# Head sums of the RWKV bonus: float32 column strips beside the key norms in place of two full-array matmuls, spread by a load from DRAM

## The chip, the cores and the metric

The kernel runs on one NeuronCore of a Trainium2 chip. The metric is the device time of one execution in microseconds (us); each comparison is between runs of both kernels on one chip. The profile of one execution tells for each engine when each instruction ran. PE is TensorE (matmuls; PEld its weight loads), DVE is VectorE, ACT is ScalarE, POOL is GpSimd, SP is SyncE, which here only issues DMAs.

## The reference, cut to what matters

One layer with two branches that read the same normalised input: 16 RWKV-7 heads of 64 channels, and a short gated convolution; then one output projection and a final norm. There are 512 frames behind 16 meta tokens. The part that the change touches is the bonus of the RWKV branch, and beside it stands the norm of the keys:

```python
hn = _rmsnorm(h_res, norm_in_g[l])
P = hn @ w_in[l]                       # 2048 -> r, k, v, gates, low-rank inputs, convolution
...
kk = (k * k_k[l]).reshape(bsz, L, H, N)
kk = kk / jnp.maximum(jnp.linalg.norm(kk.astype(jnp.float32), axis=-1, keepdims=True), 1e-12)
k = k * (1.0 + (a - 1.0) * k_a[l])
...
y = _rwkv7_recurrence(...)             # S_t = S diag(w) - (S kk)(kk a)^T + v k^T, y = S r
yn = (yn * lnx_g[l] + lnx_b[l])        # per-head norm of y
bonus = jnp.sum(rh * kh * r_k[l], axis=-1, keepdims=True) * vh
y_a = (yn + bonus.reshape(bsz, L, D_RWKV)) * jax.nn.silu(g_r)
...
h_res = h_res + mix @ w_out[l]
```

So for each frame and head there is one sum over 64 channels of r k r_k, and this one number multiplies the 64 channels of v.

## The kernel before

**Two streams on PE.** Activations lie with 128 channels on the partitions and the frames along the free dimension; two heads (a *pair*) make one 128-channel tile, so there are eight pairs, numbered 0 to 7. The input projection is the generator `mains()`: one tile of 128 output channels after another (`k`, `r`, `v`, `g` for the pairs, `B`, `C`, `h`, `gc` for the convolution). Each weight quarter is split into a high and a low half (L151 on ACT, L152 on DVE, rows `w<-wr`), which lie in a ring of six buffers, and three matmul passes follow (`xh`, `xl` against the high half, `xh` against the low one): 24 matmuls of some 256 columns for most tiles (L353), 12 of 512 columns for `B` and `gc` (L368). All other work of PE, `prepare(i)` for a pair, `invert` for two pairs, `recur` for the recurrence, is woven into this stream by hand: `fill(ns)` runs the projection for as many nanoseconds of PE work (by a fixed rate per column) before the next piece. The order of PE is thus written out; for ACT, DVE, POOL and SP a scheduler makes the order when the program is built. A step handed to `later(ns, fn)` enters the program once the projection has run that much further. Each engine works its queue strictly in order.

**A pair.** `prepare(i)` makes the chunk operands `ar` and `bk`, then multiplies r in place by half of r_k and by the scaled keys (L735, out `r`). The key norms need sums over each head: `key_norms` (L786) squares k into `sq` (576 columns) and adds up over the 64 channels of a head by four matmuls with a 128x32 slice of the constant 0/1 matrix in `cs`. The four take a quarter of the columns each (144) and stand side by side in the array, by `tile_position=(0, 32*j)`, so that each writes 32 partitions of the PSUM bank `z[0]`; rows 0 to 15 of a strip are one head, 16 to 31 the other. They run as plain float32. ACT copies the strips out (L781, `n2`, shown as `n`), two DMAs store them (`sn`, L685), one DMA loads them back in another layout (`nd`), for the inversion of small triangular blocks that DVE does line by line (L855 to L888, tile `y`). `z` is the pair of banks that the next projection tile will use; in it stand also a first small product (`ar`, `bk`, L766), and in some pairs the second level of the inversion (L1007, L1025, L1029).

**The bonus before.** The product in `r` is split into a high half on ACT and a low half on DVE (`split`, L663: rows `rk_h` L665 and `rk_l` L666, 128x512), both are multiplied with a 128x128 matrix `ones` that adds within a head and at once copies the sum to all 64 partitions of the head (L820, L821, tile `zb`), ACT copies the result over `r` (L822), DVE multiplies it by v (L919), and SP stores it to `rbd[i]` for the end of the kernel (L920). The zero strip of the next v is written by POOL (L465) once v was read.

**The end.** After the projection (last tile `gc`), the output projection runs in 56 blocks of matmuls (`M`, `P`, `Q`, L1383) on split weights (`o`, `x`, `wo`, L1338 to L1352) and split activations (`S`, L1295); then come the final norm and the stores.

Of the kernel before, what the change touches and what calls it, by code (L numbers as in the profile page):

```python
# [9 lines left out]
F32 = mybir.dt.float32  # L10
F32R = mybir.dt.float32r
I32 = mybir.dt.int32
AF = mybir.ActivationFunctionType
ALU = mybir.AluOpType
# [4 lines left out]
P = 128  # L19
DM = 2048  # L20
KT = DM // P
SEQ = 512
META = 16
L = SEQ + META
CH = 64
NCH = SEQ // CH + 1
LP = NCH * CH
# [5 lines left out]
C_ID, C_GM, C_BM, C_ON = 0, 128, 384, 512  # L33
# [11 lines left out]
    tr=3200, lev=3000, cp=4200, out=1500, begin=19500, p=2900, u=2900, s=4200, mid=1000, last=3700, mix=2600,  # L45
# [44 lines left out]
def hymba_kernel(ctx: ExitStack, tc: tile.TileContext, xt, xtok, front, w_in, w_out, pv, lup, cst, msk, gf, out):  # L90
    nc = tc.nc
    ctx.enter_context(tc.manual_schedule(engines={mybir.EngineType.PE}))
    cp = ctx.enter_context(tc.tile_pool(name="cp", bufs=1))
    dp = ctx.enter_context(tc.tile_pool(name="dp", bufs=2, space=DRAM))
# [3 lines left out]
    cs = cp.tile([P, C_N], F32, name="cs")  # L98
# [6 lines left out]
    rbd = [dp.tile([P, SEQ], F32, tag=f"rbd{j}", name=f"rbd{j}", bufs=1) for j in range(NPAIR)]  # L105
# [6 lines left out]
    def col(off, i=0):  # L112
        return pvt[:, off + i : off + i + 1]
# [55 lines left out]
    xp = ph1.enter_context(tc.tile_pool(name="xp", bufs=1))  # L169
# [3 lines left out]
    rst = xp.tile([P, 4], F32, name="rst")  # L173
    rsx = cq.tile([P, 2 * META], F32, name="rsx")
    la = cq.tile([P, 2, L], F32R, name="la")
    ones = xp.tile([P, P], F32R, name="ones")
    omm = xp.tile([P, 33], F32, name="omm")
    hv = xp.tile([P, 6, 8], F32, name="hv")
    hl = cp.tile([P, 2, 8], F32, name="hl")
# [3 lines left out]
    pi = ph1.enter_context(tc.tile_pool(name="pi", bufs=1, space=PSUM))  # L183
# [5 lines left out]
    def tr(name, dt=F32):  # L189
        return cq.tile([P, LP], dt, tag="tr", name=name, bufs=5)  # L190
# [122 lines left out]
    with tc.issue_after(head):  # L313
        nc.vector.tensor_scalar(
            out=omm, in0=pvt[:, V_MU : V_MU + 33], scalar1=-1.0, scalar2=1.0, op0=ALU.mult, op1=ALU.add
        )
        for d, off in (
# [4 lines left out]
                out=d, in0=pvt[:, off : off + 8], scalar1=0.5, scalar2=None, op0=ALU.mult  # L322
            )
        nc.vector.tensor_scalar(
            out=hv[:, 4], in0=pvt[:, V_KA : V_KA + 8], scalar1=-0.5, scalar2=1.0, op0=ALU.mult, op1=ALU.add
        )

    nc.scalar.copy(ones, cs[:, C_BM : C_BM + P])
    FULL = ((0, 272), (272, L))
    TAIL = ((14, 272), (272, L))  # L330
    REAL = ((META, L),)
# [44 lines left out]
    def next_banks():  # L376
        what, i = plan[state["tile"] + 1]
        return [pm.tile([P, 512], F32, tag="main", name=f"ps_{what}{i}_{r}") for r in range(2)]
# [217 lines left out]
    def later(ns, fn):  # L596
        pending.append((clock[0] + ns, fn))
        pending.sort(key=lambda e: e[0])
# [16 lines left out]
    def fill(ns):  # L615
        while ns > 0:
            seen = len(ready)
            t = step()
            if t is None:
                return  # L620
            ns -= t
            if len(ready) > seen:
                ns += FW["evac"]
# [23 lines left out]
    def ahead():  # L647
        return tc.high_priority(offset=AHEAD)

    def c3(t):  # L650
        return t.rearrange("p (c s) -> p c s", s=CH)
# [7 lines left out]
        nc.vector.tensor_tensor(out=lo, in0=raw, in1=hi.bitcast(F32), op=ALU.subtract)  # L659
        return hi, lo  # L660

    def split(t, name, n):
        hi = tr(f"{name}_h", F32R)[:, 0:n]  # L663
        lo = tr(f"{name}_l", F32R)[:, 0:n]
        nc.scalar.copy(hi, t)  # L665
        nc.vector.tensor_tensor(out=lo, in0=t, in1=hi.bitcast(F32), op=ALU.subtract)  # L666
        return hi, lo

    heads = [(h, slice(64 * h, 64 * h + 64), slice(64 - 64 * h, 128 - 64 * h)) for h in range(2)]

    place = [(i % 2) * 4 + i // 2 for i in range(NPAIR)]
# [11 lines left out]
    def behind(dst, src):  # L683
        with tc.issue_after(state["dma"]):
            nc.sync.dma_start(dst, src)  # L685
# [5 lines left out]
    def second_level(z):  # L691
        return [t[:, 256:512].rearrange("p (q k s) -> p q k s", q=2, s=32) for t in z]

    def prepare(i):
# [22 lines left out]
            out=bk[:, :, 0], in0=c3(k), scalar=hv[:, 2, i : i + 1], in1=c3(te), op0=ALU.mult, op1=ALU.mult  # L717
# [3 lines left out]
            out=ta, in0=ta, scalar1=hv[:, 3, i : i + 1], scalar2=hv[:, 4, i : i + 1], op0=ALU.mult, op1=ALU.add  # L721
        )
        nc.vector.scalar_tensor_tensor(
            out=ar[:, :, 0], in0=c3(k), scalar=col(V_KK, i), in1=e1[:, :, 0:CH], op0=ALU.mult, op1=ALU.mult
# [6 lines left out]
        r = got["r", i]  # L731
        nc.vector.tensor_tensor(
            out=ar[:, 1:NCH, 1], in0=c3(r), in1=e1[:, 1:NCH, 1 : CH + 1], op=ALU.mult
        )
        nc.vector.scalar_tensor_tensor(  # L735
            out=r, in0=r, scalar=hv[:, 5, i : i + 1], in1=ta[:, CH:LP], op0=ALU.mult, op1=ALU.mult
        )

        sq = tr(f"sq{i}")
        nc.scalar.activation(sq, k, AF.Square, scale=col(V_KK, i))  # L740
        rh, rl = split(r, f"rk{i}", SEQ)
        fill(FW["gram_b" if p else "gram"] + FW["meta"].get(i, 0))

        late = state["step"] > 48
# [16 lines left out]

        def gram_meta():
            z = early or next_banks()
            norms = key_norms(z[0][:, 96 : 96 + NS]) if late else None
            for h, hs, ho in heads:
                nc.tensor.matmul(  # L766
                    z[h][:, 0:META],
                    bk[hs, 0, h : h + 2, :].rearrange("p a s -> p (a s)"),
                    ar[hs, 0, 0, 0:META],
                    start=True, stop=True,  # L770
                )
            norms = norms if late else key_norms(z[0][:, 96 : 96 + NS])
            if p and "levels" in state:
                state["out"] = state.pop("levels").pop(0)(second_level(z))
            with ahead():
                for h in range(2):
                    nc.vector.tensor_tensor(
                        out=gt[:, h, 0, 0:META], in0=z[h][:, 0:META], in1=gmask[:, h, 0:META], op=ALU.mult
                    )
            with ahead():  # L780
                nc.scalar.copy(n2, norms)  # L781
            if "out" in state:
                state.pop("out")()
            state["banks"] = z

        def key_norms(z):  # L786
            for j in range(4):
                nc.tensor.matmul(
                    z[32 * j : 32 * j + 32], cs[:, C_BM + 48 : C_BM + 80], sq[:, j * NS : (j + 1) * NS],
                    start=True, stop=True, tile_position=(0, 32 * j),  # L790
                )
            return z
# [11 lines left out]

        NS = LP // 4
        n2 = tr(f"n2{i}")[:, 0:NS]
        if late:
            gram_meta()
        za = [pz.tile([P, 4, P], F32, tag="tz", name=f"g{i}_1_{h}") for h in range(2)]
# [3 lines left out]
        if not late:  # L813
            gram_meta()
# [1 line left out]
        masked(zc, 5, 9)  # L816
        fill(FW["gram2"] - FW["meta"].get(i, 0))

        zb = pi.tile([P, SEQ], F32, tag="ser", name=f"zb{i}")
        nc.tensor.matmul(zb, ones[:, 0:P], rh, start=True, stop=False)  # L820
        nc.tensor.matmul(zb, ones[:, 0:P], rl, start=False, stop=True)  # L821
        nc.scalar.copy(r, zb)  # L822
        fill(FW["misc"])


# [4 lines left out]
        sg = dp.tile([SCR], F32, tag="sg", name=f"sg{i}")  # L830
        sn = dp.tile([2 * LP], F32, tag="sn", name=f"sn{i}")
        sx = scr_x[i % 2]

        def rows(t, h):
            return bass.AP(tensor=t.tensor, offset=t.offset + h * NCH * 4 * BLK, ap=[[CH, CH], [4 * BLK, NCH], [1, CH]])
# [3 lines left out]

        for h in range(2):  # L840
            behind(sn[h * LP : (h + 1) * LP].rearrange("(j s) -> j s", s=NS), n2[16 - 16 * h : P : 32])
        for h in range(2):
            behind(rows(sg, h), gt[64 * h : 64 * h + 64, h, :, 0:CH])
        NB = 8 * NCH
# [20 lines left out]
        def sub(x, r0, c0, dims):  # L865
            return bass.AP(tensor=x.tensor, offset=x.offset + r0 * 16 + c0, ap=[list(x.ap[0])] + dims)

        for m in (2, 4, 8):
            for b in range(16 // (2 * m)):
# [4 lines left out]
                    out=pq,  # L874
                    in0=sub(d, o, o + m, [[16, m], [0, m], [1, m]]),
                    in1=sub(y, o + m, o + m, [[0, m], [1, m], [16, m]]),
                    op=ALU.mult,
                )
                nc.vector.tensor_reduce(
                    out=tq.rearrange("p (i j) -> p i j", i=m), in_=pq, op=ALU.add, axis=AX.X  # L880
                )
                nc.vector.tensor_tensor(
                    out=pq,
                    in0=sub(y, o, o, [[16, m], [0, m], [1, m]]),
                    in1=bass.AP(tensor=tq.tensor, offset=tq.offset, ap=[list(tq.ap[0]), [0, m], [1, m], [m, m]]),
                    op=ALU.mult,
# [19 lines left out]
        for h, hs, ho in heads:  # L906
            for b in range(2):
                for a in range(2):
                    later(9000 + 900 * (4 * h + 2 * b + a), lambda h=h, b=b, a=a: nc.sync.dma_start(
                        bass.AP(  # L910
                            tensor=bd.tensor,
                            offset=bd.offset + (h ^ a) * (NCH - 1) * CH * NPAIR * P + place[i] * P + 64 * h + 32 * b,
                            ap=[[NPAIR * P, 32], [32 * NPAIR * P, 2 * NCH - 2], [1, 32]],
# [2 lines left out]
                    ))  # L916
        until("v", i)
        v = got["v", i]
        nc.vector.tensor_tensor(out=r, in0=r, in1=v[:, CH:LP], op=ALU.mult)  # L919
        later(12500, lambda: nc.sync.dma_start(rbd[i], r))  # L920
        fill(FW["v"])

        vs = cq.tile([P, NCH, CH], F32, tag="vs", name=f"vs{i}")
# [1 line left out]
        for b in range(4):  # L925
            for t in range(2):
                later(14000 + 1000 * (2 * b + t), lambda b=b, t=t: nc.sync.dma_start(
                    bass.AP(
                        tensor=vd.tensor,
                        offset=vd.offset + (64 * (1 - b // 2) + 32 * t) * NPAIR * CH + place[i] * CH + 32 * (b % 2),  # L930
                        ap=[[NPAIR * CH, 32], [P * NPAIR * CH, NCH], [1, 32]],
# [427 lines left out]
    def here(t, n):  # L1359
        return xa[t][:, n * 512 : (n + 1) * 512] if n < 2 else xb[n - 2][:, t]  # L1360
# [153 lines left out]
    z = {}  # L1514
# [55 lines left out]
    with tc.manual_schedule(engines={mybir.EngineType.DVE, mybir.EngineType.Activation, mybir.EngineType.Pool}):  # L1570
# [16 lines left out]
        for part in range(2):  # L1587
            cols = slice(256 * part, 256 * part + 256)
            for jj in range(8):
                hi, lo = right[(1, "M2", jj // 2), jj % 2]  # L1590
# [4 lines left out]
            h = here(1, 2)[:, cols]  # L1595
# [70 lines left out]
```

## Time and profile before

| | |
|---|---|
| three runs | 991.49, 991.8, 992.1 us; median 991.8 us |
| the profiled execution | 991.71 us in all, 989.6 us from the first to the last instruction |
| granted TensorE clock in it | 0.998 |
| PE busy | 980.0 us (99%) |
| DVE, ACT, POOL busy | 706.8 us (71%), 390.6 us (39%), 127.8 us (13%) |
| DMA | 176.91 MB, mean 179 GB/s |

Busy time is time with an instruction of the program in work. Matmuls are pipelined, and their ends are modelled: what a matmul costs PE is read from the start of one to the start of the next. A line number Lnnn is that of the kernel before. In rows that end on something like `[1.38 <-DMA nd<-sn]` the engine stood idle for 1.38 us until the landing of that DMA. Rows of SPq, and of ACTq where a DMA is named, are the issue of a DMA by that engine's queue, not the transfer. A mark `x8` counts instructions; a float32 matmul has two records.

### The profile page before, as it was taken

The page shows a single profiled execution, that of the slowest core. Times are in us where ns is not written, and L with a number is a line of the kernel's source. Part 1 is how long each engine was busy: PE and PEld are TensorE (multiplying, and loading weights), DVE is VectorE, ACT ScalarE, POOL GpSimd, SP SyncE. Part 2 cuts the span into 40 slices and gives each one's busy share as a digit, 9 for nine tenths or more (in the row PEclk, how much of TensorE's full clock was granted, in tenths as well). Part 3 has the DMA queues.
Part 4 walks back from the last instruction along what each step waited for, and adds up shares of the span by engine and source line. Part 5 has one row for each costly group of instructions (what it writes and reads, how often), then busy time and mean ns, then how long its engine had stood idle before and what let it go on. Part 6 is the DMA issues. An engine that isn't in the chain of part 4 may idle for free.

```text
span 989.6 us, 23395 instructions
## 1 busy us (share of the span) xinstructions
PE 980.0 (99%) x9511; PEld 907.5 (92%) x9511; DVE 706.8 (71%) x1413; ACT 390.6 (39%) x731; POOL 127.8 (13%) x242
## 2 busy tenths in 40 slices
PE   9999999999999999999999999999999999999996
PEld 9999999999998999998999998889889898788885
DVE  7777966578675779653778654365756697998896
ACT  7553432343322434322434323232323335446454
POOL 0110302112010111010111010011211102001001
PEclk9999999999999999999999999999999999999999
DMA  9526586246684375853275856999886697697554
GB/s 325 156 91 152 143 206 164 82 130 145 153 199 150 92 187 123 209 153 115 89 176 125 202 143 192 275 253 258 229 267 167 181 300 182 180 320 189 150 128 171
DMA packets 205532, 176.91 MB, mean 179 GB/s; under 512 B 138544, under 2 KB 168048, under 8 KB 205040
## 3 DMA queue, kind: packets, MB, share of 16 engines
q1 hardware_dynamic: 202832, 166.50, 60.2%
q0 software_dynamic: 2304, 8.39, 5.0%
q8 instruction: 75, 1.23, 0.5%
q10 hardware_dynamic: 288, 0.52, 0.1%
q14 instruction: 33, 0.27, 0.1%
HBM read 139.02 MB, written 36.35 MB: 177 GB/s over the span
## 4 chain that ended last, share of the span: by engine, by line
PE 95%; DVE 3%; ACT 1%; issue 1%; DMA 0%; DVEq 0%; POOL 0%; ACTq 0%
PE ps_v L353 9%; PE ps_h L353 9%; PE ps_C L353 9%; PE ps_g L353 9%; PE ps_B L368 9%; PE ps_gc L368 9%; PE ps_k L353 8%; PE ps_r L353 8%; PE M L1383 5%; PE P L1383 4%; PE Q L1383 2%; PE g L755 2%; PE ps_k L368 1%; PE ps_r L368 1%; PE ps_lora L368 1%; PE zy L1141 1%
## 5 line engine op out<-in xcount | busy, mean ns | idle before, releaser
L151 ACT CAST w<-wr 128x512 fp32r<-128x512 f32 x252 | 153.7, 619 | 285.1 <-PE ps_C L353 44.8
L152 DVE TENSOR_TENSOR w<-wr,w 128x512 fp32r<-128x512 f32 x252 | 174.8, 705 | 116.4 <-ACT w L151 115.5
L353 PE MATMUL ps_v<-xh,w 128*128 128x256 f32 (+2 forms) x512 | 84.0, 285 | 0.0
L368 PE MATMUL ps_B<-xh,w 128*128 128x512 f32 x256 | 83.4, 394 | 0.0
L353 PE MATMUL ps_h<-xh,w 128*128 128x256 f32 (+2 forms) x512 | 81.7, 281 | 0.0
L353 PE MATMUL ps_g<-xh,w 128*128 128x256 f32 (+2 forms) x512 | 81.4, 281 | 0.0
L368 PE MATMUL ps_gc<-xh,w 128*128 128x512 f32 x256 | 81.2, 392 | 0.0
L353 PE MATMUL ps_C<-xh,w 128*128 128x256 f32 (+2 forms) x512 | 80.8, 280 | 0.0
L353 PEld LDWEIGHTS ps_v<-xh,w 128*128 128x128 f32 x512 | 73.9, 188 | 0.3
L353 PE MATMUL ps_k<-xh,w 128*128 128x256 f32 (+1 forms) x448 | 73.4, 285 | 0.0
L353 PEld LDWEIGHTS ps_g<-xh,w 128*128 128x128 f32 x512 | 72.0, 189 | 0.6 <-issue 0.2
L353 PE MATMUL ps_r<-xh,w 128*128 128x256 f32 (+1 forms) x448 | 72.5, 280 | 0.0
L353 PEld LDWEIGHTS ps_h<-xh,w 128*128 128x128 f32 x512 | 72.1, 189 | 0.3
L353 PEld LDWEIGHTS ps_C<-xh,w 128*128 128x128 f32 x512 | 71.8, 189 | 0.2
L353 PEld LDWEIGHTS ps_k<-xh,w 128*128 128x128 f32 x448 | 64.7, 188 | 0.4
L353 PEld LDWEIGHTS ps_r<-xh,w 128*128 128x128 f32 x448 | 63.5, 189 | 0.4 <-issue 0.2
L353 PE MATMUL ps_h<-xl,w 128*128 128x256 f32 x256 | 57.3, 281 | 0.0
L368 PEld LDWEIGHTS ps_gc<-xh,w 128*128 128x128 f32 x256 | 47.8, 188 | 10.0
L368 PEld LDWEIGHTS ps_B<-xh,w 128*128 128x128 f32 x256 | 47.8, 188 | 9.7
L353 PE MATMUL ps_C<-xl,w 128*128 128x256 f32 x256 | 56.2, 280 | 0.0
L353 PE MATMUL ps_v<-xl,w 128*128 128x256 f32 x256 | 55.8, 278 | 0.0
L353 PE MATMUL ps_g<-xl,w 128*128 128x256 f32 x256 | 55.4, 278 | 0.0
(382 smaller groups left out, 2144.5 us busy)
## 6 DMA issues: line engine op xcount, KB each, us to landing
wr<-in_w_in_dram SPq DMA_DIRECT2D x126, 512.0 KB
ct<-opd SPq DMA_DIRECT2D x72, 192.0 KB
wo<-in_w_out_dram SPq DMA_DIRECT2D x24, 512.0 KB
x<-in_w_out_dram POOLq DMA_DIRECT2D x16, 512.0 KB, 5.6
opd<-ar SPq DMA_DIRECT2D x8, 576.0 KB
opd<-gt SPq DMA_DIRECT2D x16, 288.0 KB
bd<-bt SPq DMA_DIRECT2D x64, 64.0 KB
bw<-bd SPq DMA_DIRECT2D x16, 256.0 KB
```

What stands on the lines that cost most here:

```text
L151: nc.scalar.copy(hi, rq)
L152: low[q] = eng.tensor_tensor(out=lo, in0=rq, in1=hi.bitcast(F32), op=ALU.subtract).ins
L353: nc.tensor.matmul(ps[r][:, 0 : b - a], ww[:, k * P : (k + 1) * P], xx[:, kt, a:b], start=(kt == 0 and n == 0), stop=(kt == KT - 1 and n = ...
L368: nc.tensor.matmul(ps[r], ww[:, w], xx[:, kt, a:b], start=(kt == 0 and n == 0), stop=(kt == KT - 1 and n == 2))
L755: nc.tensor.matmul(z[h][:, c - c0], bk[hs, c, h : h + 2, :].rearrange("p a s -> p (a s)"), ar[hs, c].rearrange("p a s -> p (a s)"), start= ...
L1141: nc.tensor.matmul(zy[e][hs if e else ho, k], t[hs, o : o + CH], x, start=(n == 0), stop=(n == 2))
L1383: nc.tensor.matmul(bank[s], left(prod, jj, m, s), w, start=(jj == 0 and n == 0), stop=(jj == 7 and n == 2))
```

## The change

The bonus is added up in the way of the key norms. Right behind the four matmuls on `sq` stand four on `r` (128 columns each, float32, the same 128x32 slice of `cs`, the same four strips), which write the other bank, `z[1]`. ACT copies these strips (128x128, tile `nb`) behind the norms. On ACT's own queue two DMAs store the 2 x 512 sums to DRAM (`sb`), and a third loads them back so that every partition of a head gets the 512 sums of its head, straight into `r` (256 KB in SBUF from 4 KB in DRAM). The product with v comes when the projection has run 14.5 us further (`later(14500, ...)`), the store to `rbd` after 17.5 us instead of 12.5. The split of `r`, the matrix `ones` and the two full-array matmuls go.

```diff
-    nc.scalar.copy(ones, cs[:, C_BM : C_BM + P])
...
         sq = tr(f"sq{i}")
         nc.scalar.activation(sq, k, AF.Square, scale=col(V_KK, i))
-        rh, rl = split(r, f"rk{i}", SEQ)
...
             z = early or next_banks()
-            norms = key_norms(z[0][:, 96 : 96 + NS]) if late else None
+            if late:
+                norms, bonus = sums_of(z)
...
-            norms = norms if late else key_norms(z[0][:, 96 : 96 + NS])
+            if not late:
+                norms, bonus = sums_of(z)
...
             with ahead():
                 nc.scalar.copy(n2, norms)
+                nc.scalar.copy(nb, bonus)
...
-        def key_norms(z):
+        def sums_of(z):
+            return head_sums(z[0][:, 96 : 96 + NS], sq, NS), head_sums(z[1][:, 96 : 96 + P], r, P)
+
+        def head_sums(z, x, n):
             for j in range(4):
                 nc.tensor.matmul(
-                    z[32 * j : 32 * j + 32], cs[:, C_BM + 48 : C_BM + 80], sq[:, j * NS : (j + 1) * NS],
+                    z[32 * j : 32 * j + 32], cs[:, C_BM + 48 : C_BM + 80], x[:, j * n : (j + 1) * n],
                     start=True, stop=True, tile_position=(0, 32 * j),
                 )
             return z
...
+        nb = tr(f"nb{i}")[:, 0:P]
...
-        zb = pi.tile([P, SEQ], F32, tag="ser", name=f"zb{i}")
-        nc.tensor.matmul(zb, ones[:, 0:P], rh, start=True, stop=False)
-        nc.tensor.matmul(zb, ones[:, 0:P], rl, start=False, stop=True)
-        nc.scalar.copy(r, zb)
         fill(FW["misc"])
...
+        sb = dp.tile([2 * SEQ], F32, tag="sb", name=f"sb{i}")
...
+        for h in range(2):
+            later(1000, lambda h=h: nc.scalar.dma_start(
+                sb[h * SEQ : (h + 1) * SEQ].rearrange("(j s) -> j s", s=P), nb[16 * h : P : 32]
+            ))
+        later(7000, lambda: nc.scalar.dma_start(r, bass.AP(tensor=sb.tensor, offset=sb.offset, ap=[[SEQ, 2], [0, CH], [1, SEQ]])))
...
-        nc.vector.tensor_tensor(out=r, in0=r, in1=v[:, CH:LP], op=ALU.mult)
-        later(12500, lambda: nc.sync.dma_start(rbd[i], r))
+        later(14500, lambda: nc.vector.tensor_tensor(out=r, in0=r, in1=v[:, CH:LP], op=ALU.mult))
+        later(17500, lambda: nc.sync.dma_start(rbd[i], r))
```

What that makes of the order, at three places (the number at a tile's end is that of its buffer; line numbers of the changed kernel are a few lower). PE at pair 4, before, where the bonus of the pair stands amid the projection tile `ps_k`:

```order
L353 MATMUL ps_k_0_4653<-xl,w_4431 128x256
L353 MATMUL ps_k_0_4653<-xh,w_4431 128x256 x2
L353 MATMUL ps_k_0_4653<-xl,w_4431 128x256
L353 MATMUL ps_k_0_4653<-xh,w_4431 128x256
L820 MATMUL zb_4808<-rk_h,ones 128x512
L821 MATMUL zb_4808<-rk_l,ones 128x512
L353 MATMUL ps_k_0_4653<-xh,w_4431 128x256
L353 MATMUL ps_k_0_4653<-xl,w_4431 128x256
```

PE at pair 4 in the changed kernel, at the key norms (`sq`), some 8 us earlier in the stream:

```order
L1006 MATMUL ps_k_0_4655<-xm_4191,gt_3489 32x32 x2
L1006 MATMUL ps_k_1_4656<-xm_4191,gt_3489 32x32 x2
L784 MATMUL ps_k_0_4655<-sq_4567,cs 32x144 x4
L784 MATMUL ps_k_1_4656<-r_4544,cs 32x128 x4
L757 MATMUL ps_k_0_4655<-ar_4393,bk_4394 128x16
L757 MATMUL ps_k_1_4656<-ar_4393,bk_4394 128x16
```

The two rows of `zb` are gone from the projection; one row of four strips stands behind that of the norms, and the rows around it are as before.

ACT at pair 5, before: the copy of the norms, casts of weights, the copy of `zb`:

```order
L781 COPY n_5321<-ps_g_0_5342 128x144
L151 CAST w_5280<-wr_5275 128x512
L151 CAST w_5312<-wr_5310 128x512
L822 COPY r_5121<-zb_5454 128x512
L151 CAST w_5315<-wr_5310 128x512
```

ACT at pair 5 in the changed kernel:

```order
L773 COPY n_5325<-ps_g_0_5347 128x144
L774 COPY nb_5326<-ps_g_1_5348 128x128
L837 DMA sb_5488<-nb_5326 4x128 x2
L151 CAST w_5284<-wr_5279 128x512
L840 DMA r_5128<-sb_5488 128x1x512
L151 CAST w_5316<-wr_5314 128x512
L151 CAST w_5319<-wr_5314 128x512
```

Three DMA issues stand between the casts, the third with one cast between it and the stores that it reads; in pairs 2, 4 and 6 it stands right behind the stores.

DVE at pair 5, before: the product with v stands behind two low halves of weights, ahead of the reading of the tile `ps_g`:

```order
L152 TENSOR_TENSOR w_5280<-wr_5275,w_5280 128x512
L152 TENSOR_TENSOR w_5312<-wr_5310,w_5312 128x512
L919 TENSOR_TENSOR r_5121<-r_5121,v_5261 128x512
L404 TENSOR_TENSOR pr_g_5533<-ps_g_0_5283,rs 128x256
L403 TENSOR_TENSOR ex<-ps_g_1_5284,rst 128x4
```

DVE at pair 5 in the changed kernel:

```order
L152 TENSOR_TENSOR w_5284<-wr_5279,w_5284 128x512
L918 TENSOR_TENSOR r_5128<-r_5128,v_5265 128x512
L152 TENSOR_TENSOR w_5316<-wr_5314,w_5316 128x512
L402 TENSOR_TENSOR pr_g_5539<-ps_g_0_5287,rs 128x256
L401 TENSOR_TENSOR ex<-ps_g_1_5288,rst 128x4
```

In spite of the later entry into the program, the product stands at nearly the same place of DVE's queue (here one low half earlier), and now it reads what a load brings. Elsewhere on DVE the low half `rk_l` is gone from each pair and small steps of the inversion have changed places with their neighbours; on SP the store `rbd<-r` stands a few DMAs later.

More of the change, by code (lines that the diff above doesn't have):

```diff
@@ L175, in hymba_kernel @@
     la = cq.tile([P, 2, L], F32R, name="la")
-    ones = xp.tile([P, P], F32R, name="ones")
     omm = xp.tile([P, 33], F32, name="omm")
@@ L660, in lora_up @@
         return hi, lo
[L662 to L667, printed above, removed]
     heads = [(h, slice(64 * h, 64 * h + 64), slice(64 - 64 * h, 128 - 64 * h)) for h in range(2)]
```

## The prediction

> **What bounds the kernel now.** I read the page first, then the chain of work that ended last, then PE's own waits.
>
> ```profile
> PE 980.0 (99%) x9511; PEld 907.5 (92%) x9511; DVE 706.8 (71%) x1413; ACT 390.6 (39%) x731; POOL 127.8 (13%) x242
> PE 95%; DVE 3%; ACT 1%; issue 1%; DMA 0%; DVEq 0%; POOL 0%; ACTq 0%
> ...
> PE pwarm L202 <- DVE cold L199: 1.0, 1, 1.0
> PE M L1383 <- DVE o L1352: 0.3, 1, 0.3
> ```
>
> The first row is busy time, the second the chain by engine, the last two all waits of PE that the trace names: 1.3 us in the whole run, one at its start, one in the output projection. PE is not merely busy, it is never kept waiting in the stretch where the eight pairs are prepared (84 to 547 us, by the rows below). So there a microsecond of PE work removed is a microsecond won, and work on DVE, ACT or SP counts only if it makes PE wait.
>
> How far PE is from waiting shows in who waits for it:
>
> ```profile
> ACT w L151 <- PE ps_C L353: 44.8, 23, 5.0
> DVE w L152 <- ACT w L151: 118.5, 89, 4.7
> ...
> 104.19 16.39 PE ps_g L353 x141
> ```
>
> The casts of weights wait mostly until PE gives a buffer of the ring back, and DVE waits for the casts. The last row, of the chain, gives 16.39 / 141 = 0.116 us a matmul, so a quarter of 24 lasts 2.8 us; with six buffers full, five quarters or some 14 us of weights lie ready. I take 10 us as the usual lead.
>
> **What goes from PE.** PE around `zb` in pair 7, then the removed work by line:
>
> ```profile
> 545.88 0.40 PE L353 MATMUL ps_g<-xh,w 128*128 128x256 f32 x2
> 546.12 0.39 PE L820 MATMUL zb<-rk_h,ones 128*128 128x512 f32 x1
> 546.35 0.39 PE L821 MATMUL zb<-rk_l,ones 128*128 128x512 f32 x1
> 546.58 0.28 PE L353 MATMUL ps_g<-xl,w 128*128 128x256 f32 x1
> ...
> L665 ACT CAST rk_h<-r x8: 620/621/624, 76.6 to 529.7; 128x512 fp32r<-128x512 f32 x8
> L666 DVE TENSOR_TENSOR rk_l<-r,rk_h x8: 677/690/694, 78.4 to 530.4; 128x512 fp32r<-128x512 f32 x8
> L822 ACT COPY r<-zb x8: 579/587/589, 89.0 to 546.8; 128x512 f32<-128x512 f32 x8
> ```
>
> From the start of L820 to that of the next projection matmul are 546.58 - 546.12 = 0.46 us, with weight loads hidden; times eight pairs this is 3.68 us of PE. DVE loses 8 x 0.69 = 5.5 us, ACT 8 x (0.62 + 0.59) = 9.7 us: worth nothing in time, because PE did not wait for either. The one conversion of `ones` at the start is worth nothing for the same reason.
>
> **What comes to PE.** Four strips of 128 columns in float32, which are eight records in two rounds of four. The trace has the nearest thing twice:
>
> ```profile
> 252.42 1.28 PE L755 MATMUL g<-ar,bk 64*128 64x128 f32 x20
> 253.54 0.30 PE L766 MATMUL ps_C<-ar,bk 64*128 64x16 f32 x4
> 253.76 0.45 PE L788 MATMUL ps_C<-sq,cs 128*32 128x144 f32 x8
> 254.15 0.22 PE L1025 MATMUL ps_C<-xT,tm 32*32 32x32 f32 x2
> ```
>
> Low end: the 20 records of L755 are ten rounds (two heads side by side) of 128 float32 columns in 253.54 - 252.42 = 1.12 us, so 0.112 us a round; two make 0.22. High end: the whole group of the norms, 254.15 - 253.76 = 0.39 us, as if the new strips paid again for entering and leaving the shape. Two rounds of 144 columns at the rate of L755 are 0.25 us, so 0.14 of the 0.39 are that entry and exit, which the new strips share with the norms just ahead. I take 0.26, near the low end, with a little for four records a round instead of two: 8 x 0.26 = 2.08 us.
>
> [...]
>
> **What comes to the other engines, and what covers it.**
>
> ```profile
> L781 ACT COPY n<-ps_C x2: 278/278/279, 124.2 to 258.1; 128x144 f32<-128x144 f32 x2
> 984.39 0.38 ACTq L1564 DMA_DIRECT2D out_dram<-xa  x1
> ...
> 495.00 1.12 SPq L685 DMA_DIRECT2D sn<-n  x2
> 497.44 0.34 SPq L685 DMA_DIRECT2D nd<-sn  x1
> ...
> 266.81 0.53 SPq L685 DMA_DIRECT2D nd<-sn  x1
> 267.39 0.50 SPq L159 DMA_DIRECT2D wr<-in_w_in_dram  x1
> ...
> 269.02 0.17 DVE L855 TENSOR_SCALAR nd<-nd 72x16 f32<-72x16 f32 x1 [1.38 <-DMA nd<-sn]
> ...
> 271.32 1.18 ACT L151 CAST w<-wr 128x512 fp32r<-128x512 f32 x2 [3.77 <-DMA wr<-in_w_in_dram]
> ```
>
> ACT: the copy of `nb` at most the 0.28 us of `n`. An issue takes 0.38 us on its queue here, 0.34 to 0.56 on SP, so three are 1.0 to 1.7 us. The third waits for the stores: the norms' two stores started at 495.00, and the load that reads them began at 497.44, so 2.44 us from the first store, 1.32 after both issues. In pairs 2, 4 and 6 nothing stands between: ACT is held some 0.28 + 2.44 + 0.38 = 3.1 us, and the casts behind are late by part of that. The lead of 10 us covers it.
>
> DVE: the product with v waits for the load. Two transfers bound it: 2.2 us for the small `nd` (266.81 to 269.02), 3.9 us for 512 KB of weights (267.39 to 271.32); 256 KB from a few rows I put at 3. From the copy of `nb`, the sums are in `r` after 0.28 + 2.44 + 3 = 5.7 us at least, 6 to 7 with a cast between. Pair 5, where the product's place moved up:
>
> ```profile
> 393.79 0.28 ACT L781 COPY n<-ps_g 128x144 f32<-128x144 f32 x1 [3.23 <-DVE gt L777]
> 396.80 0.69 DVE L152 TENSOR_TENSOR w<-wr,w 128x512 fp32r<-128x512 f32 x1 [0.68 <-ACT w L151]
> 399.58 0.69 DVE L152 TENSOR_TENSOR w<-wr,w 128x512 fp32r<-128x512 f32 x1 [2.09 <-ACT w L151]
> 400.38 0.69 DVE L919 TENSOR_TENSOR r<-r,v 128x512 f32<-128x512 f32 x1
> ```
>
> The norms were copied by 394.07, so `r` is there at 400 to 401; DVE would come to the product at 397.5 and stand there for 2.5 to 3.5 us, of which 2.09 it stood idle before anyway. Behind it wait one low half of weights and the reading of `ps_g`; a low half late by 1 us is covered by the lead. POOL's zero strip of the next v waits for the product as it did before, and what stands behind it on POOL is some microsecond later; SP's store of `r`, 5 us later in the program, finds the product done. I cost all of this at nothing; without the lead, each pair would pay the 1 to 3.5 us that are late.
>
> The reading of `nb` holds the bank `z[1]` for 0.28 us more, before the next tile writes it; PE's list of waits shows none on that bank now.
>
> **The sum.** -3.68 + 2.08 = -1.60 us. The profiled execution took 991.71 us, so 990.1; it lay 0.09 under the median of 991.8, by which the forecast is 990.2 us. With the two ends for the strips it is 991.8 - 3.68 + 1.79 = 989.9 and 991.8 - 3.68 + 3.12 = 991.2; strips that hid wholly behind the norms would give 988.1. About 0.2%, 2.0 us, is what a measurement of this kernel can tell from no change, so the forecast lies just within it.
>
> **Rivals.** *The strips cost less:* the exit of the norms (part of the 0.14 us) may overlap the new rounds, or each round may take less than L755's. Every pair at 0.21 us or under gives 990.0 - 0.2 = 989.8 or less, down to 988.1. For it: entry and exit are already paid; against: no row shows a 128-column round under 0.112.
>
> *The change brings PE nothing:* the array is emptied between the two groups, or the gain is eaten at the one wait in the output projection, where the path leaves PE:
>
> ```profile
> 816.87 10.90 PE ps_gc L368 x48
> ...
> 863.58 0.61 DVE o L1352
> ...
> 864.24 5.27 PE M L1383 x22
> ```
>
> If what paces DVE there stood still in time, PE would come 1.6 us earlier and wait 1.6 longer: 991.8. Against it: that chain starts when PE ends `ps_gc` at 816.87 + 10.90 = 827.77, and goes through DVE and ACT alone, so it moves with PE. By emptying, 991.2.
>
> *Slower:* one place has no lead. A step of the convolution kept four casts back:
>
> ```profile
> 290.63 0.73 ACT L487 ACTIVATE cv<-u,pvt 128x512 f32<-128x512 f32 x1 [10.42 <-POOL u L485]
> 291.26 2.17 ACT L151 CAST w<-wr 128x512 fp32r<-128x512 f32 x4
> 292.85 2.49 DVE L152 TENSOR_TENSOR w<-wr,w 128x512 fp32r<-128x512 f32 x4
> 293.85 0.19 PEld L368 LDWEIGHTS ps_B<-xl,w 128*128 128x128 f32 x1
> ...
> 287.20 0.68 DVE L888 TENSOR_REDUCE y<-prod 72x64 f32<-72x512 f32 x1
> 287.80 0.41 DVE L404 TENSOR_TENSOR hh<-ps_h,rs 128x256 f32<-128x256 f32 x1
> 288.65 0.16 DVE L403 TENSOR_TENSOR ex<-ps_h,rst 128x4 f32<-128x4 f32 x1 [0.44 <-PE ps_h L353]
> ```
>
> The first of these low halves is done at 292.85 + 0.68 = 293.53; by counting twelve matmuls a quarter, PE begins on it at 293.85. Its chain comes through `hh` from the inversion of pair 3 (`y`) on DVE, which ended 0.44 us before it would have held `ex` up. If the product with v, or the load's share of the transfers, makes that inversion late by more than 0.44 + 0.3 us, PE waits for the rest, and over 0.7 + 1.6 + 2.0 = 4.3 us late it is slower: 6 us late gives 990.2 + 5.3 = 995.5. For it: the inversion's small loads and the new load run in the same stretch. Against: DVE was idle for 1.38 us right at that inversion's start (the row of `nd` at 269.02), and so takes up as much of the product's delay before `y` is touched. [...]
>
> **How the numbers follow.** Forecast (strips at 0.22 to 0.39, no wait of PE) 0.55; strips cheaper 0.20; nothing gained 0.11; slower 0.14. Faster by over 0.2% is the second, 0.20; within 0.2% are the first and third, 0.66; slower 0.14. The range takes in both ends for the strips, half of the way to free strips (989.0), and a loss of 0.6 us against before (992.4); below lies some 0.05, above most of the slower case, 0.13.
>
> **What the profile after would show.** Right: from the norms' first matmul to the one behind the strips some 0.65 us, where 0.39 stood; no `zb`; PE's list of waits as short as now; DVE idle ahead of the product until a DMA `r<-sb`; ACTq rows of 0.3 to 0.6 us, the third with a wait. Wrong: 0.8 us for the two groups, PE waiting for DVE `w` near 294 us or 130 us, or a longer wait at `M`.

## The result, and the profile after

The changed kernel took 1005.78 us (median; 1004.48 to 1006.65) against 991.95 before: ratio 1.0139, 95% interval 1.0121 to 1.0156. It is 13.8 us slower, where 990.2 had been forecast and 992.4 was the upper end.

The page of the changed kernel, its busy time and the chain by engine, then the whole list of PE's waits (us in total, times, longest):

```profile
PE 983.8 (98%) x9559; PEld 909.1 (91%) x9559; DVE 700.7 (70%) x1405; ACT 381.9 (38%) x722; POOL 133.0 (13%) x242
PE 76%; DVE 11%; DMA 8%; ACT 2%; issue 2%; POOL 1%; SPq 0%; ACTq 0%; DVEq 0%; POOLq 0%
```

```profile
PE ps_B L366 <- ACT w L151: 2.6, 1, 2.6
PE ps_gc L366 <- DVE w L152: 2.0, 1, 2.0
PE ta L633 <- ACT tz L638: 2.0, 2, 1.4
PE g L745 <- DVE bk L718: 1.7, 1, 1.7
PE pwarm L201 <- DVE cold L198: 1.0, 1, 1.0
PE ps_B L366 <- DVE w L152: 0.6, 1, 0.6
PE ps_C L757 <- DVE pr_g L402: 0.5, 1, 0.5
PE M L1382 <- DVE o L1351: 0.3, 1, 0.3
```

PE no longer holds 95% of the chain but 76%, and DMA has 8%. PE waits for 10.7 us in place of 1.3 (the expectations below say 11.2, an adding error), half of it (5.2 us) where the weights of the convolution's tiles `ps_gc` (at 159 us) and `ps_B` (at 298 us) come late. PE's busy time grew by 3.8 us although its work shrank. The table of stretches says why; its columns are the stretch, the busy time of the five engines, the granted clock of PE, the DMA share and GB/s:

```profile
158.00:160.00 2.00, 1.29 (x6) 0.75 (x4) 1.97 (x4) 0.00 (x0) 0.00 (x0) 1.00 0.88 173
160.00:162.00 2.00, 0.71 (x2) 0.62 (x3) 1.83 (x5) 0.00 (x0) 1.47 (x2) 0.90 0.64 137
162.00:164.00 2.00, 2.00 (x6) 1.58 (x5) 0.00 (x0) 0.72 (x2) 1.25 (x1) 0.50 0.76 138
164.00:166.00 2.00, 2.00 (x8) 1.54 (x8) 1.93 (x3) 1.03 (x3) 0.34 (x1) 0.74 0.98 293
...
300.00:302.00 2.00, 0.67 (x2) 0.31 (x2) 1.16 (x2) 1.95 (x4) 1.04 (x4) 0.89 0.12 19
302.00:304.00 2.00, 1.37 (x3) 0.83 (x3) 2.00 (x4) 0.84 (x2) 0.29 (x2) 0.50 0.55 125
304.00:306.00 2.00, 2.00 (x6) 1.60 (x5) 1.43 (x3) 0.00 (x0) 0.00 (x0) 0.50 0.88 160
306.00:308.00 2.00, 2.00 (x6) 1.52 (x6) 0.03 (x1) 0.00 (x0) 0.00 (x0) 0.50 0.92 262
308.00:310.00 2.00, 2.00 (x9) 1.37 (x7) 0.00 (x0) 0.00 (x0) 0.00 (x0) 0.90 1.00 371
310.00:312.00 2.00, 2.00 (x69) 1.80 (x69) 0.00 (x0) 0.76 (x3) 0.14 (x1) 1.00 0.44 169
```

After the two longest waits PE ran at half its clock, for 3.4 us behind the first and 6.8 behind the second (by these rows; a stretch at 0.90 was at half for a fifth of it). So the price of a late weight is not the wait alone.

The load did not land after 3 us. In pair 1, ACT's queue and then DVE:

```profile
133.12 0.54 ACTq L840 DMA_DIRECT2D r<-sb  x1
```

```profile
142.17 0.69 DVE L918 TENSOR_TENSOR r<-r,v 128x512 f32<-128x512 f32 x1 [8.99 <-DMA r<-sb]
```

From issue to use are 9.05 us, of which DVE stood 8.99; the three low halves of weights that come next in its queue, whose casts had ended by 134.33, 135.46 and 137.27 us, began only behind the product, at 142.78. Over the run DVE stood 52.6 us at this product. Why so long is seen in the view of the DMA queues, narrowed to the time of this load's packets (134.7 to 141.7 us; packets, MB, share of 16 engines; q10 is ACT's queue):

```profile
q1 hardware_dynamic: 1197, 0.29, 18.6%
q10 hardware_dynamic: 129, 0.26, 10.9%
```

10.9% of sixteen transfer engines are 1.7 engines at a mean, and by the packet records of the trace, of these 7.0 us two packets of this queue were in work for 4.9, one for 1.9 and three for 0.2. From these numbers I put the engines that move the whole 256 KB, in 128 packets of 2 KB, at about two: an estimate, as no row names an engine.

### The profile page after: what moved, and what is told of

Read it like the earlier page. It is cut to its first block, busy times and chain, and to the rows that moved or that the text cites. A ratio compares the mean times of both kernels' runs of the same rounds, so it can differ in the third digit from the quotient of the medians.

```text
span 1002.7 us, 23476 instructions
## 1 busy us (share of the span) xinstructions
PE 983.8 (98%) x9559; PEld 909.1 (91%) x9559; DVE 700.7 (70%) x1405; ACT 381.9 (38%) x722; POOL 133.0 (13%) x242
## 4 chain that ended last, share of the span: by engine, by line
PE 76%; DVE 11%; DMA 8%; ACT 2%; issue 2%; POOL 1%; SPq 0%; ACTq 0%; DVEq 0%; POOLq 0%
PE ps_B L366 9%; PE ps_gc L366 8%; PE ps_C L351 7%; PE ps_k L351 7%; PE ps_v L351 7%; PE ps_h L351 6%; PE ps_r L351 5%; PE M L1382 5%; PE ps_g L351 4%; DMA r<-sb 4%; PE P L1382 4%; PE Q L1382 2%; DVE w L152 1%; DMA wr<-in_w_in_dram 1%; PE ps_k L366 1%
## 5 line engine op out<-in xcount | busy, mean ns | idle before, releaser
L151 ACT CAST w<-wr 128x512 fp32r<-128x512 f32 x252 | 152.5, 619 | 285.9 <-DMA wr<-in_w_in_dram 65.9
L366 PE MATMUL ps_B<-xh,w 128*128 128x512 f32 x256 | 85.7, 403 | 3.2 <-ACT w L151 2.6
```

Of the source, the lines that this page charges most:

```text
L151: nc.scalar.copy(hi, rq)
L366: nc.tensor.matmul(ps[r], ww[:, w], xx[:, kt, a:b], start=(kt == 0 and n == 0), stop=(kt == KT - 1 and n == 2))
```

## The experiments

The kernel before took 991.6 to 992.1 us beside each group of runs. Four theories were weighed: A, DVE stands at the product; B, ACT is held at the third issue; C, the slow load keeps two transfer engines from the other transfers; S, SP stands until the load has landed, since in this program the DMAs of ACT and SP take eight semaphores (counters that tell of a landing) in turn, and one of SP's next DMAs can come to the one that the load still holds. In the trace of the changed kernel 679 DMAs of SP and 26 of ACT carry the numbers 101 and 104 to 110, POOL's 16 the numbers 111 to 118; at pair 1 the load has 104, and so have the weights that SP issues at 142.21 us. D, that the strips cost PE more, and E, that a late product holds POOL up, are side theories.

**Two loads with a leading count of 64** (e1)

```diff
-        later(7000, lambda: nc.scalar.dma_start(r, bass.AP(..., ap=[[SEQ, 2], [0, CH], [1, SEQ]])))
+        for h in range(2):
+            later(7000, lambda h=h: nc.scalar.dma_start(
+                r[h * CH : (h + 1) * CH], bass.AP(..., offset=sb.offset + h * SEQ, ap=[[0, CH], [1, SEQ]])))
```

> The one load of 256 KB becomes two of 128 KB, one for each head, whose DRAM side starts with a count of 64 instead of 2; everything else is kept, so ACT issues one DMA more per pair. Theory A (the load is slow because only two of its packets run at a time, and DVE stands at the product until it lands): each load lands within 4 us of its issue instead of 8.4 to 10.5, DVE's wait at the product falls from 52.6 us to under 25, PE's waits from 11.2 us to under 4, time 989.5 to 993. Rival B (ACT is held by the issue that waits for the stores, so casts are late): one more issue, no gain, 1005 to 1008. Rival C (the traffic of stores and load delays the weights): same bytes, 1003 to 1006. Rival D (the strips cost PE more than the two full-array matmuls did): 1005.8.

989.78 us, ratio 0.9979 (0.9970 to 0.9988): faster than the kernel before, by 2.0 us. All waits of PE, then DVE's at the product (from the view of the tile `sb`: us, times), then the queues in the 3 us of the packets (127.8 to 130.8 us):

```profile
PE pwarm L201 <- DVE cold L198: 1.0, 1, 1.0
PE M L1385 <- DVE o L1354: 0.3, 1, 0.3
```

```profile
  DVE r L921: 5.9, 6
```

```profile
q10 hardware_dynamic: 160, 0.26, 36.8%
q1 hardware_dynamic: 941, 0.23, 34.4%
```

The same bytes now use 36.8% of sixteen engines, 5.9 at a mean over two loads issued 1.4 us apart, and PE waits as in the kernel before. B and D fall: ACT issues one DMA more, and the strips are the same.

**The same with a leading count of 2, and of 4** (e8, e11; only this list is changed in e1)

```diff
-ap=[[0, CH], [1, SEQ]]
+ap=[[0, 2], [0, CH // 2], [1, SEQ]]     # e8
+ap=[[0, 4], [0, CH // 4], [1, SEQ]]     # e11
```

> Two loads of one head each, as in the run that gave 989.8 us, but the DRAM side of each is written with a leading count of 2 (2 x 32 rows) instead of 64; number of DMAs, bytes, queue and waits are the same. If the leading count is what makes the load slow: 6 to 9 us from issue to landing again, 1002 to 1008. If it was the splitting into two that helped: 989.5 to 991.

> Two loads of one head each, the DRAM side with a leading count of 4 (4 x 16 rows), all else as in the two runs with 64 (989.8) and 2 (1008.7). If the count is the number of engines that share the packets: both loads have landed 4 to 6 us after the first issue, half as late as with 2; DVE's wait at the product falls to between 5 and 25 us; the time lies near the fast one, 989.5 to 995, since SP's next eight DMAs take longer than that. If only a full spread helps: 1000 to 1008.

With 2: 1008.71 us, ratio 1.0160 (1.0138 to 1.0181), just above the 1002 to 1008 that had been set for it. With 4: 989.59 us, 0.9972 (0.9961 to 0.9982). DVE's wait at the product is 44.8 us with 2, 21.0 with 4, 5.9 with 64, but only the 2 costs time. The count at the front of the DRAM side is what made the changed kernel slow: the number of DMAs, bytes, queue, order and product are the same in the three. The shares above go with it: 1.7 engines at a mean with 2 in front (the changed kernel), 5.9 with 64 (e1). Why the count sets the share, and which engines they are, no row here shows.

**Without the load; with a load that is not waited for** (e2, e3, e5)

```diff
 # e2: the load goes
 # e3: the load fills a tile that nobody reads
+        rs_ = cq.tile([P, SEQ], F32, tag="rsx", name=f"rsx{i}", bufs=1)
 # e5: the load fills a tile that only SP's later store reads
+        ru = cq.tile([P, SEQ], F32, tag="ru", name=f"ru{i}", bufs=1)
-        later(17500, lambda: nc.sync.dma_start(rbd[i], r))
+        later(17500, lambda: nc.sync.dma_start(rbd[i], ru))
```

> The load is left out, so the product with v multiplies r before it is summed; strips, copies and the two stores stay. Theory A: no wait at the product, PE's waits as before (1.3 us), and what is left is PE's own saving, 989.9 to 991.2. B and C: the third issue and the traffic are gone too, so also 990 to 992. Rival D: 1004 to 1006, as PE's work is the same as in the changed kernel.

> The load stays as it is, on ACT's queue behind the stores, but it fills a tile that nobody reads, and the product multiplies r before it is summed. Theory A: as without the load, 989.9 to 991.5. Rival B: ACT still stands for 1 us at that issue, so the time stays at 1003 to 1006. Rival C: the traffic is the same, 1003 to 1006. Rival D: 1004 to 1006.

> The load stays as it is in the changed kernel, behind the stores on ACT's queue, but fills a tile of its own that only SP's later store to rbd reads; the product multiplies r before it is summed and so waits for nothing. What the product's wait alone costs is thereby taken away. Theory A (all through the product's wait on DVE): 989.5 to 991. Theory S (SP's queue stands until the load has landed, because one of its next DMAs is counted on the same semaphore, and the weights behind it are late): 997 to 1002, with SP waiting for this load some 3 to 6 us in several pairs. Theory C (the load keeps two of the transfer engines busy for 6 us, and pieces of the other transfers wait there): also 997 to 1002, but with SP waiting for other transfers.

e2: 989.42 us, 0.9979 (0.9971 to 0.9988): PE's own saving, a little below the 989.9 to 991.2 set for it. e3 does not test this: its tile took a name that another tile of the pool already had, so the loads waited until that one was last read, and all eight then stood one behind the other on ACT's queue from 531.9 to 588.3 us. Its 1032.25 us tell nothing on A or C. e5 is the run that e3 was to be: 1004.35 us, 1.0114 (1.0098 to 1.0131), more than any of the three theories had set. DVE waits for no load, and still nearly the whole loss is there, with SP waiting 9.5 us for the load. Theory A, with which I came out of the first comparison, is not needed for the loss.

**The product held back on DVE, with the slow load and with fast ones** (e4, e10)

```diff
-        later(14500, lambda: nc.vector.tensor_tensor(out=r, in0=r, in1=v[:, CH:LP], op=ALU.mult))
-        later(17500, lambda: nc.sync.dma_start(rbd[i], r))
+        def with_v():
+            with tc.issue_after(low[2 * state["next"] - 1 - 4]):
+                nc.vector.tensor_tensor(out=r, in0=r, in1=v[:, CH:LP], op=ALU.mult)
+        later(14500, with_v)
+        later(26500, lambda: nc.sync.dma_start(rbd[i], r))
 # e10: and the two loads of e1
```

> The load stays as slow as it is, but the product with v is held on DVE's queue behind a low half of weights that stands 9 to 45 instructions further on, and its store to rbd comes 9 us later in the program. Theory A: the load has landed when DVE comes to the product, its wait there falls from 52.6 us to under 10, PE's waits to under 4 us, time 990 to 993. B, C and D: nothing that they name is changed, 1003 to 1006. A further rival E (POOL's zero strip of the next v now waits longer for the product, and the work behind it on POOL is late in its turn): PE waits at new places, 995 to 1003.

> Control for the kernel with the slow load on ACT's queue and the product held back (999.7): the same, but as two loads with a leading count of 64. If holding the product back costs nothing itself, this is as fast as the two fast loads with the product in its old place, 989 to 991, and all of the 10 us of that kernel come from the slow load by S and C. If holding it back costs (theory E: POOL's zero strip and what is behind it), 993 to 999.

The added lines let the product go only behind a low half of the weights that stands further on in DVE's queue: in e4 the first product starts at 114.0 us, in the changed kernel at 98.3. e4 took 999.70 us, 1.0096 (1.0078 to 1.0114); e10 989.72, 0.9978 (0.9969 to 0.9988). So holding the product back costs nothing, and takes away only a part of the loss: some 10 us remain with a slow load for which DVE does not wait. e4 and e5 ought to be alike by that and lie 4.7 us apart; both vary by 6 to 8 us between runs, and their orders on DVE differ. That difference stays open. Part of the spread goes with PE's clock: of e4's six executions four took 999.2 to 999.8 us at a mean granted clock of 0.994 to 0.996, two took 1004.2 and 1004.9 us at 0.992, and the trace is of the last. The 999.70 us lie in the range that was set for E, but e10 rules E out.

**The load on POOL's queue** (e6, e7, e9): the two loads of e8 issued by POOL with the product in its old place (e6) or held back (e7), and e7 with a leading count of 64 (e9).

```diff
-            later(7000, lambda h=h: nc.scalar.dma_start(
+            later(7000, lambda h=h: nc.gpsimd.dma_start(
```

> The load goes to POOL's queue, which counts its DMAs on semaphores of its own, as two loads of one head with a leading count of 2 (so as slow as before); the product with v waits for them in its old place. S: SP no longer waits for the load, and what is left is the product's wait on DVE, 992 to 998. C: 1003 to 1006, as in the changed kernel. A: 1003 to 1006 as well, since DVE waits as long.

> As the kernel with the load on POOL's queue, but with the product held back behind a later low half on DVE, as in the run before. Neither DVE nor SP waits for the load, which is still slow and still keeps its transfer engines busy. S together with A: 989.5 to 992. C: 997 to 1001, as with the product alone held back (999.7).

> Control for the kernel with the slow loads on POOL's queue and the product held back (999.4): the same kernel, but the DRAM side of the loads starts with a count of 64, so they are fast. S (what cost time was SP's stand behind the load, and 999.4 without it was only POOL's own standing at its DMAs): no change, 998 to 1001. C (the slow load's hold on two transfer engines costs by itself): 989.5 to 993.

e6 1032.97 us, e7 999.39 (1.0065 to 1.0100), e9 989.48 (0.9963 to 0.9984). With a slow load POOL itself was held: in e7, the two loads of pair 3:

```profile
264.87 0.76 POOL L841 DMA_DIRECT2D r<-sb  x1 [3.08 <-DMA sb<-nb]
271.59 0.66 POOL L841 DMA_DIRECT2D r<-sb  x1 [5.97 <-DMA sn<-n]
```

The second stood 6 us behind the first, and what is behind it on POOL with it (in e9 0.38 us). So e7 does not tell S from C. e6 is a miss of all the ranges.

**One load more that nobody waits for, on POOL's queue and on ACT's, slow and fast** (e12 to e15), added to e1:

```diff
+        extra = cq.tile([120, SEQ], F32, tag="extra", name=f"extra{i}", bufs=1)
+        later(7000, lambda: nc.gpsimd.dma_start(extra, bass.AP(..., ap=[[0, 2], [0, 60], [1, SEQ]])))   # e12
 # e13: ap=[[0, 120], [1, SEQ]];  e14, e15: the same two by nc.scalar
```

> The fast kernel (two loads with a leading count of 64, 989.8), plus one further load per pair on POOL's queue, of 120 rows of 2 KB of the same sums into a tile that nobody reads, with a leading count of 2. The extra load keeps two transfer engines busy for some 5 us like the load of the changed kernel, but its semaphore is not one that SP's DMAs take, and nobody waits for it. C (other transfers are late behind it): 995 to 1001. S (only waiting for its semaphore costs): 989.5 to 991.5, as with a leading count of 120.

> Control: the same extra load on POOL's queue with a leading count of 120, so spread over many engines. Both theories: 989.5 to 991.5; what is more is the price of POOL standing at the extra issue.

> The same extra load, leading count 2, on ACT's queue right behind the two fast loads. It is counted on one of the semaphores that SP's DMAs take in turn, and nobody reads its tile. S: SP stands until it has landed, as in the changed kernel, 997 to 1005. C alone: the same as on POOL's queue.

> Control: the extra load on ACT's queue with a leading count of 120. Both theories: 989.5 to 991.5, as ACT's third issue behind the stores is 0.5 us more and its casts have a lead.

| extra load | leading count 2 | leading count 120 |
|---|---|---|
| POOL's queue | 1002.08 us, 1.0104 (1.0088 to 1.0119) | 989.55 us, 0.9983 (0.9974 to 0.9992) |
| ACT's queue | 1001.92 us, 1.0106 (1.0088 to 1.0124) | 989.67 us, 0.9980 (0.9972 to 0.9989) |

So C is enough by itself, as far as it says that a slow load makes other transfers late; on which engines they wait, no row shows. On POOL's queue the load has a semaphore that SP does not take (111 to 118 in the changed kernel's trace), nobody reads its tile, POOL stands about as long at its issue until `sb` has landed in both forms (32.8 us in e12, 32.4 in e13), and the slow form costs the same 12 us as on ACT's queue; with a leading count of 120 it costs nothing on either. S is to be seen (SP's list of waits has 4.5 us for the extra load in e14, and 11 us for the load in the changed kernel), but beside C it adds nothing measurable in e14.

How it reaches PE: SP's queue at pair 1, first with the fast extra load (e13), then with the slow one (e12). `sn` is the store of the key norms, `nd` the load that reads it, `sg` a store of the inversion's operands, `wr` the next weights.

```profile
128.81 0.73 SPq L676 DMA_DIRECT2D sn<-n  x1
129.64 1.29 SPq L676 DMA_DIRECT2D sg<-gt  x2
132.55 0.32 SPq L676 DMA_DIRECT2D nd<-sn  x1
132.97 1.28 SPq L159 DMA_DIRECT2D wr<-in_w_in_dram  x1
```

```profile
131.38 0.72 SPq L676 DMA_DIRECT2D sn<-n  x1
132.20 2.10 SPq L676 DMA_DIRECT2D sg<-gt  x2
138.09 0.33 SPq L676 DMA_DIRECT2D nd<-sn  x1
138.52 0.37 SPq L159 DMA_DIRECT2D wr<-in_w_in_dram  x1
```

From the store to the load that must wait for it are 3.74 us in the one, 6.71 in the other, and the weights behind on the same queue go with it. The store is small: by the packet records of the traces its four packets of 576 bytes take 0.03 us each. In e13 they start 2.0 to 2.7 us after the issue, in e12 1.8 to 6.1 us after it. In the chain of waits of e12 these are the pieces (start, us, what):

```profile
131.38 6.65 DMA sn<-n
138.09 0.33 SPq L676
138.52 3.88 DMA wr<-in_w_in_dram
142.47 0.63 ACT w L151
143.12 0.69 DVE w L152
```

In sum SP waited 24.0 us for `sg` and 10.2 for `sn` in e12, 5.8 and 9.8 in e13; ACT's casts waited 68.8 us for weights, against 32.8. The changed kernel has the same signs: 15.8 and 14.2 us, and 65.9 for weights (25.5 in the kernel before). But e11, which costs nothing, has them too: 11.1 and 13.7 us, and 57.9 for weights, while PE waits no more than before. These sums alone do not give the price; as I read the traces, it is paid only where the work comes later than PE's lead.

In the changed kernel the way is not that of e12 alone. Its chain of waits goes four times through the load itself, at pairs 0, 1, 3 and 6. Two pieces of it at pair 1, then SP's waits there and at pair 3, then the chain at pair 6:

```profile
133.12 9.03 DMA r<-sb
142.21 4.23 DMA wr<-in_w_in_dram
```

```profile
SPq L159 <- DMA r<-sb: 5.1, 1, 5.1
SPq L676 <- DMA r<-sb: 3.0, 1, 3.0
```

```profile
510.50 10.50 DMA r<-sb
521.64 1.29 DVE w L152 x2
```

At pairs 1 and 3, ahead of the two long waits for weights, SP stands for the load (S); at pairs 0 and 6 DVE stands at the product (A), and PE's waits for `g` (1.7 us) and for `ta` at 530 us (1.4) follow. The runs do not divide the loss among the three ways. What they show is that the count of 2 causes it, that C alone is enough for 12 us, and that without A most of it is still there (some 10 us in e4, nearly all in e5).

## Why the prediction was wrong

- *PE's terms were right.* Pair 6, the group of the norms before, then with the strips behind it (e1):

```profile
493.67 0.45 PE L788 MATMUL ps_k<-sq,cs 128*32 128x144 f32 x8
494.05 0.40 PE L766 MATMUL ps_k<-ar,bk 64*128 64x16 f32 x4
```

```profile
491.98 0.45 PE L784 MATMUL ps_k<-sq,cs 128*32 128x144 f32 x8
492.25 0.40 PE L784 MATMUL ps_k<-r,cs 128*32 128x128 f32 x8
492.58 0.40 PE L757 MATMUL ps_k<-ar,bk 64*128 64x16 f32 x4
```

  0.38 us became 0.60: a strip group costs 0.22, the low end, not the 0.26 taken (0.21 to 0.23 in the eight pairs). That makes 8 x (0.46 - 0.22) = 1.9 us saved, and e1 measured 2.0. That 0.14 us of the norms' 0.39 are an entry and exit which the strips share was my estimate, and no run shows it as a thing of its own; what the runs show is that the strips, in another PSUM bank and in the same shape, add the 0.22 us of two rounds of 0.112 us and not the 0.39 of a whole group.
- *The step that failed* is the load: "256 KB from a few rows I put at 3". It was bounded by a small load (2.2 us) and by 512 KB of weights (3.9), and both have many rows at the front of the DRAM side, where this one has a count of 2. From issue to product it took 9 us, and from the copy of `nb` to the product 12.5 us at pair 1, where 5.7 to 7 had been counted. The bound above was none.
- *The cover was looked for in the wrong place.* "DVE: the product with v waits for the load" and "I cost all of this at nothing" asked only who waits for the load itself. By e5 and e4 the loss does not hang on that wait, though the trace of the changed kernel shows it largest (52.6 us). By e12 some 12 us are lost through transfers that have nothing to do with the bonus: the store of the norms lands late, SP stands at the load that reads it, and the weights behind it are late. In the changed kernel SP stood for the load itself as well, another term that was put at nothing.
- *The slower rival* named the right place (293.85 us, the convolution without a lead; PE waited there for 2.6 + 0.6 us) and "the load's share of the transfers" as one cause, at 0.14. It missed the second place (`ps_gc`, 159 us), and the half clock behind the two longest waits (3.4 and 6.8 us).
- *The account of the 13.1 us of span* (1002.7 - 989.6): waits of PE +9.4 (10.7 - 1.3), half clock up to 5.1 (3.4 us and 6.8 us at half the rate, by the granted clock of all stretches of 2 us behind the two waits), less 1.9 for the strips; these make 12.6, and 0.5 is spread over rows I did not trace.
- *The sign that I had set* for the load ("DVE idle ahead of the product until a DMA `r<-sb`") came true, and would have passed as a full explanation had e5 not been run.

## What to carry to other kernels

Before a DMA is priced by its bytes, look at the first count of its DRAM side: with 2 there, 256 KB took 9 us and held up transfers that others waited for; as two loads with 4 or 64 in front the change gave the 2 us that its matmuls promised. A slow transfer that nobody waits for can cost nearly as much as one that is waited for (12 us here), if a queue that carries weights stands at another small transfer. A wait that grew in the list of waits is a suspect, not a cause: take it away alone and see whether the time comes back.

## What was not expected of the hardware

In the changed kernel PE's clock fell to half after waits of 2.0 and 2.6 us, and not after those of 1.7 and 1.4. The length of the wait alone does not decide it: in e5 it fell after a wait of 1.56 us (at 448 us) and not after one of 1.60 (at 533 us), and in e8 not after one of 2.17 us (at 174 us). What else decides, the place of the wait in time or what PE did ahead of it, was not tried. Nor do the runs show why a count of 4 at the front costs nothing (e11) and a count of 2 costs 12 to 19 us (e12, e8): with 4, the load still took until 4.4 us after DVE was ready for it.
